# Laying out the softmax statistics directly behind the last join of a weight pair

## The chip, the cores and the metric

The kernel runs on one core of a Trainium2 chip. The metric is the time of one execution on the device in microseconds (us), the median of several runs. Engines are named as in the profile: PE is TensorE (matrix products; PEld its weight loads), DVE is VectorE (elementwise work and reductions), ACT is ScalarE (activations and copies), POOL is GpSimd, SP is SyncE (here a queue for transfers).

## The reference

A trunk of two layers over 512 positions of width 1024, in float32. Layer 0 mixes tokens with dilated attention, layer 1 with causal pooling; a SwiGLU feed-forward part of width 2816 follows each. The change lies in the attention: for each of 8 head slots there are three groups with dilations 1, 4 and 16, each with its own queries, keys and values, and the three outputs are merged by their softmax denominators:

```python
for g, (window, dil) in enumerate(ATTN_PAIRS):          # (128,1), (512,4), (2048,16)
    o, lse = dilated_window_attention(qkv[:, :, g, 0], qkv[:, :, g, 1], qkv[:, :, g, 2], window, dil, slopes[g])
    outs.append(o)
    lses.append(lse)
wts = jax.nn.softmax(jnp.stack(lses, axis=0), axis=0)
o = jnp.sum(wts[..., None] * o, axis=0).reshape(B, S, ATTN_WIDTH)
return o.astype(h.dtype) @ w_out
```

## The kernel before

**Products.** Every float32 product is done in three matmuls with a high and a low part of each factor (`mult`, L391 to L393: weight high by data high, weight high by data low, weight low by data high). Weight matrices come from HBM as raw tiles and are split by ACT (high part, `whi`, L96) and DVE (low part, `wlo`, L97).

**Pairs.** Most weights are taken as a `Pair`: two column blocks whose product is formed with seven half products in place of eight (`seven` for queries, keys and the even heads' values, `values12` for other values). A pair goes through four weight steps: `blocks`, `sums`, `more` (two DVE additions, L173 and L174, then a split) and `last` (a split of a half tile, `halfhi` and `halflo`). The steps of all pairs stand in one queue; `pump` takes the next one if its ring of buffers has room, and issues loads that fit. In `seven` each of the seven products is followed by `behind(i)`, which calls `pump` once and then whatever attention work is registered for that turn in `after[i]`. DVE adds the half products together; the last of these additions, the last join (L446 in `seven`, L594 in `values12`), is put on the list `mark`.

**Heads.** For each head h, `scores0` and `scores12` compute scores and their maxima and sums, the statistics `st` (DVE reductions, and sums that ACT writes beside its exponentials, L667). One group of statistics has its positions in another order across partitions than the other, so `merge` exchanges them: DVE spreads `st` out into the tile `far` (L680, multiplying with the mask `place`), TensorE multiplies it with the matrix `swap` (L684), DVE picks the result apart (L687, L690), and a short chain of small operations ends in the factors `co` for the probabilities. `turn0` and `turn12` transpose the probabilities and `output` multiplies them with the values. This work of head h−1 is spread over the three pairs of head h by `between(h, g)`: `merge(h-1)` stands at turn 2 of the first of them. An even head ends with the values pair that goes through `seven` (tiles `vt`), an odd one with `values12`. The last head has its `merge` at turn 3 of its own `values12`.

**Order.** The program is written as one stream; a planner sets each engine's queue from it before the run: by its own estimate of times, an engine gets, among the instructions that would be ready, the one that stands first in the program. On the chip each engine takes its queue in order. `tc.issue_after(x)` adds that instructions of x's engine within the block come behind x in that queue, without waiting for x to finish. In the kernel before, `merge` uses this to keep `far` behind the most recent last join:

```python
far = apool.tile([P, 4 * NT, NT], F32, tag="b12", name="far")
with tc.issue_after(mark[-1].ins) if mark else nullcontext():
    nc.vector.tensor_mul(far, ...)
```

`far` lives in the buffer of `b12` (the position biases that `scores12` of the same head has read, and that POOL writes anew for the next head, L624). PSUM banks are handed out by `ps()` in a ring of eight (`RING`).

Of the kernel before, what the change touches and what calls it, by code (L numbers as in the profile page):

```python
# [8 lines left out]
F32 = mybir.dt.float32  # L9
# [6 lines left out]
P = 128  # L16
# [11 lines left out]
NT = S // P  # L28
# [23 lines left out]
def trunk(ctx: ExitStack, tc: tile.TileContext, xT, norms, w_first, w_qk, w_qkp, w_v0, w_v0p, w_v12, w_out, w_pair, w_down, w_down0, w_down1, w_down2, w_pin, w_pgrp,  # L52
          consts, ident_in, invcnt_in, outT):
    nc = tc.nc
# [17 lines left out]
    def ps(tag=None):  # L72

        if tag is None:
            if turn["ring"] is None:
                tag = "ps"
            else:
                tag = RING[turn["ring"] % len(RING)]
                turn["ring"] += 1
        return psum.tile([P, S], F32, tag=tag, name=tag, bufs=BANKS[tag])  # L80
# [59 lines left out]
    class Pair:  # L140
# [38 lines left out]
        def last(self):  # L179
            self.made("l", "half", self.c.t, 1)  # L180
            self.c.done()
# [108 lines left out]
    def give(key):  # L290
        free.append(held.pop(key))
# [85 lines left out]
    mark = []  # L377
# [17 lines left out]
    def part(unit, name):  # L395
        while name not in unit.w:
            pump(must=True)
        return unit.w[name]

    def seven(T, one, two, scratch, after={}, blocks=False):  # L400


        unit, = units.popleft()
        into, left, right = by_block if blocks else in_place, slice(0, 1), slice(1, 2)

        def again(v):
            return v.unsqueeze(1).to_broadcast([P, 2, H2])

        p1, p26, p45, p73 = ps(), ps(), ps(), ps()

        def behind(i):
            pump()
            for f in after.get(i, ()):
                f()

        w = part(unit, "b")
        mult(p1[:, :H2], w, 0, T, "11")
        first, sums = scratch("first"), scratch("sums")
        nc.scalar.copy(first[:, :H2], p1[:, :H2])
        behind(0)  # L420
        mult(p26[:, :H2], w, 1, T, "21")
        w.done()
        behind(1)
        w = part(unit, "s")
        mult(p45[:, H2:], w, 0, T, "1")
        behind(2)
        mult(p73[:, :H2], w, 1, T, "3")
        w.done()
        behind(3)
        w = part(unit, "m")  # L430
        mult(p26[:, H2:], w, 0, T, "2")
        nc.vector.tensor_add(into(one), p26, again(first[:, :H2]))
        behind(4)
        mult(p73[:, H2:], w, 1, T, "22")
        w.done()
        if blocks:
            for a in (left, right):
                nc.vector.tensor_add(in_place(sums, a), in_place(p73, a), into(one, right))
        else:
            nc.vector.tensor_add(sums, p73, again(one[:, H2:]))  # L440
        behind(5)
        w = part(unit, "l")
        mult(p45[:, :H2], w, 0, T, "4")
        w.done()
        nc.vector.tensor_sub(into(two), p45, again(sums[:, :H2]))
        mark.append(nc.vector.tensor_sub(into(one, right), sums[:, H2:], p45[:, H2:]))  # L446
        behind(6)

    def chain(T, share, left, right, low, high, behind=None):

# [66 lines left out]
    with tc.tile_pool(name="opool", bufs=1) as opool:  # L517
        early = opool.tile([P, HEADS, S], F32R, tag="o", name="early")
        with tc.tile_pool(name="apool", bufs=1) as apool:
# [4 lines left out]
            A = {}  # L524
# [73 lines left out]
            VT = []  # L598
# [48 lines left out]
            def scores12(h):  # L647
# [19 lines left out]
                    nc.scalar.activation(v, v, AF.Exp, bias=nm[:, 1, r:r + 1], accum_out=st[:, 0, 1, 1, r:r + 1])  # L667
                A[h]["s12"] = s12

            def merge(h):  # L670


                st, s0, s12 = A[h]["st"], A[h]["s0"], A[h]["s12"]
                mx = apool.tile([P, 2, NT], F32, name="mx")
                ex = apool.tile([P, 2, 2, NT], F32, name="ex")
                dd = apool.tile([P, 2, 2, NT], F32, name="dd")
                co = apool.tile([P, 2, NT], F32, name="co")
                far = apool.tile([P, 4 * NT, NT], F32, tag="b12", name="far")
                with tc.issue_after(mark[-1].ins) if mark else nullcontext():
                    nc.vector.tensor_mul(far, st[:, 0].rearrange("p a s b -> p (a s b)").unsqueeze(2).to_broadcast(  # L680
                        [P, 4 * NT, NT]), place[:, None].to_broadcast([P, 4 * NT, NT]))
                p = ps()
                for a in range(2):
                    nc.tensor.matmul(p[:, a * 32:(a + 1) * 32], swap,  # L684
                                     far[:, (1 - a) * 8:(2 - a) * 8].rearrange("p s r -> p (s r)"), start=True, stop=True)

                nc.vector.tensor_mul(far.rearrange("p (q r) b -> p q r b", r=NT),  # L687
                                     p[:, :64].rearrange("p (q b r) -> p q r b", b=NT, r=NT),
                                     place[:, None, None].to_broadcast([P, 4, NT, NT]))
                nc.vector.tensor_reduce(st[:, 1].rearrange("p a s r -> p (a s r)"), far, axis=AX.X, op=OP.add)  # L690
                nc.vector.tensor_max(mx, st[:, 0, :, 0, :], st[:, 1, :, 0, :])
                nc.vector.tensor_sub(ex, st[:, :, :, 0, :], mx[:, None].to_broadcast([P, 2, 2, NT]))
                nc.scalar.activation(ex, ex, AF.Exp)
                nc.vector.tensor_mul(dd, ex, st[:, :, :, 1, :])
                nc.vector.tensor_add(mx, dd[:, 0], dd[:, 1])
                nc.vector.reciprocal(mx, mx)
                nc.vector.tensor_mul(co, ex[:, 0], mx)
                for b in (1, 2, 3, 0):
                    nc.vector.tensor_scalar(s0blk(s0, b), s0blk(s0, b), co[:, 0, b:b + 1], None, op0=OP.mult)
                for r in range(NT):  # L700
                    v = s12[:, r].rearrange("p g k -> p (g k)")
                    nc.scalar.activation(v, v, AF.Copy, scale=co[:, 1, r:r + 1])
# [53 lines left out]
            H, T, o = {}, {}, []  # L756
# [35 lines left out]
            def scratch(name):  # L792
                return apool.tile([P, S], F32, tag="scratch", name=name, bufs=3)
# [11 lines left out]
            for k in range(KC):  # L805
# [5 lines left out]
                s = slice(k % 2 * NF * P, (k % 2 + 1) * NF * P)  # L811
# [17 lines left out]
            def later(f, *a):  # L829
                return lambda: f(*a)  # L830

            def between(h, g):

                if g == 0:
                    return {2: [later(merge, h - 1)], 4: [later(turn_values, h - 1)] if h > 1 else []} if h % 2 else {
                        1: [later(output, h - 2)], 2: [later(merge, h - 1)]}
                if g == (2 if h == 1 else 1):
                    return {0: [later(turn0, h - 1)], 2: [later(turn12, h - 1)], 4: [later(scores0, h)]}
                return {} if h % 2 else {2: [later(output, h - 1)]}
# [8 lines left out]
            place = apool.tile([P, NT], F32, name="place")  # L848
            nc.sync.dma_start(place, consts[:, 5 * P:])
            VT[:] = [scratch("vt") for c in range(2)]  # L850
            for c in range(2):
                p = product(0)
# [6 lines left out]
            for h in range(1, HEADS):  # L859
                for g in range(3):  # L860
                    if h == 1 and g < NSOLO:
                        for c in range(2):
                            evac(h, 2 * g + c, product(0))
                        for fs in between(h, g).values():
                            for f in fs:
                                f()
                    else:
                        for c in range(2):
                            QKV[h, g, c] = apool.tile([P, S], F32, name=f"qk{g}{c}")
                        seven(T, QKV[h, g, 0], QKV[h, g, 1], scratch, between(h, g), g == 0)  # L870
                if h == 1:
                    whole = opool.tile([P, HEADS, S], F32, tag="o", name="o")
                    o.extend(whole[:, h, :] for h in range(HEADS))
                if h == HEADS - 1:
                    for key in [key for key in held if key[0] == "t"]:
                        give(key)
                    X[:] = [x_tile(k) for k in range(KC)]
                    for k in range(KC):
                        nc.gpsimd.dma_start(X[k], xT[:, k, :])
                if h % 2 == 0:  # L880
                    VT[:] = [apool.tile([P, S], F32, tag=tag, name="vt") for tag in ("row", "o0")]
                    seven(T, *VT, scratch, {0: [later(scores12, h)]}, True)
                elif h < HEADS - 1:
                    QKV[h // 2, 12, 2] = values12({0: [later(scores12, h)]})
                else:
                    QKV[h // 2, 12, 2] = values12({0: [later(scores12, h)], 1: [later(halve, 0), later(halve, 1)],
                                                   2: [later(halve, 2), later(halve, 3)], 3: [later(merge, h)],
                                                   4: [later(halve, 4), later(halve, 5)]})
            for k in range(KC):
                give(("h", k))  # L890
# [1 line left out]
            last = HEADS - 1  # L892
# [478 lines left out]
```

## Time and profile before

| | |
|---|---|
| time, median of 3 runs | 1255.39 us (1254.78 to 1256.69) |
| time of the profiled execution | 1255.31 us |
| its span, first to last instruction | 1253.5 us |
| granted TensorE clock | 0.998 |
| TensorE busy | 1238.3 us (99%) |
| VectorE busy | 1012.8 us (81%) |
| ScalarE busy | 679.9 us (54%) |
| DMA, mean over the span | 151 GB/s |

The times of rows are microseconds from the start of the span. A row of a timeline has the start, the duration, the engine, the line, the operation, the tile written and the tiles read, the shapes and the count; in brackets stands how long the engine was idle before it and what ended that. A row of the waits has the waiting instruction, the instruction that it waited for, the total in us, the number of times and the longest. A row of the windows has the stretch and its length, then the busy time of each engine with its number of instructions, the granted clock, the share of DMA time and GB/s. The attention heads' part that the change touches lies between about 60 and 440 us; the feed-forward part, the pooling layer and the second feed-forward part follow.

### The profile page before, as it was taken

To read this page: it belongs to the slowest core of one execution; us is meant where nothing else is said; L and a number is where in the kernel's file an instruction comes from. 1 tells how busy PE (TensorE), PEld (TensorE's weight loads), DVE (VectorE), ACT (ScalarE), POOL (GpSimd) and SP (SyncE) were. 2 spreads that over 40 slices of the span, in tenths; PEclk is the share of its full clock that TensorE was granted. 3 is DMA by queue.
4 is the path that set the end of the run, shared out by engine and by line. 5 is a ranking of instruction groups with operands and counts; after the bars stand their busy time and mean duration, and the time that the engine had idled before them with its cause. 6 is when DMAs were issued, how large, how long until landed. Compare 5 with 4: busy or idle time off the path is not lost. (4 is left out here: it accounts for less than half of the span.)

```text
span 1253.5 us, 23247 instructions
## 1 busy us (share of the span) xinstructions
PE 1238.3 (99%) x9072; PEld 1173.6 (94%) x9072; DVE 1012.8 (81%) x1687; ACT 679.9 (54%) x1171; POOL 157.7 (13%) x147
## 2 busy tenths in 40 slices
PE   9999999999999999999999999999999999999997
PEld 7889999999999998889999999988788999999997
DVE  7987787878778747698778888798989877888876
ACT  6444554445455535466466556554446646656652
POOL 1111111111111010101111111100220111111100
PEclk9999999999999999999999999999999999999999
DMA  8336556655755443437777687553144777677742
GB/s 280 109 92 171 136 143 149 165 133 146 186 141 140 138 152 119 109 94 184 184 186 170 177 191 178 137 198 123 51 118 100 190 189 179 147 192 205 169 123 68
DMA packets 76719, 189.91 MB, mean 151 GB/s; under 512 B 7600, under 2 KB 15936, under 8 KB 76608
## 3 DMA queue, kind: packets, MB, share of 16 engines
q1 hardware_dynamic: 51696, 142.26, 35.8%
q0 software_dynamic: 24336, 45.63, 22.2%
q8 instruction: 71, 1.16, 0.4%
q10 hardware_dynamic: 576, 0.52, 0.1%
q14 instruction: 40, 0.33, 0.1%
HBM read 186.29 MB, written 2.10 MB: 150 GB/s over the span
## 5 line engine op out<-in xcount | busy, mean ns | idle before, releaser
L96 ACT ACTIVATE whi<-raw 128x1024 fp32r<-128x1024 f32 (+2 forms) x315 | 318.7, 1016 | 254.0 <-PE seed L392 78.5
L97 DVE TENSOR_TENSOR wlo<-raw,whi 128x1024 fp32r<-128x1024 f32 (+2 forms) x315 | 366.6, 1167 | 108.0 <-ACT whi L96 107.2
L158 POOL DMA_DIRECT2D raw<-w_pair x34 | 41.1, 1209 | 312.3 <-DMA raw<-w_pair 61.9
L391 PE MATMUL sum<-tt,whi 128*128 128x256 f32 x272 | 77.0, 283 | 1.6 <-ACT seed L473 0.8
L392 PE MATMUL sum<-tt,whi 128*128 128x256 f32 x272 | 76.6, 282 | 0.0
L393 PE MATMUL sum<-tt,wlo 128*128 128x256 f32 x272 | 76.4, 281 | 0.0
L96 ACT ACTIVATE halfhi<-rawhalf 128x512 fp32r<-128x512 f32 (+1 forms) x87 | 53.1, 612 | 19.5 <-PE sum L392 12.2
L173 DVE TENSOR_TENSOR raw<-raw 128x512 f32<-128x512 f32 (+1 forms) x87 | 57.5, 661 | 1.8 <-issue 1.7
L174 DVE TENSOR_TENSOR raw<-raw 128x512 f32<-128x512 f32 (+1 forms) x87 | 57.5, 661 | 0.2
L97 DVE TENSOR_TENSOR halflo<-rawhalf,halfhi 128x512 fp32r<-128x512 f32 (+1 forms) x87 | 57.4, 661 | 0.0
L158 POOL DMA_DIRECT2D raw<-w_down x24 | 28.9, 1206 | 213.8 <-DMA raw<-w_down 75.4
L391 PEld LDWEIGHTS sum<-tt,whi 128*128 128x128 f32 x272 | 51.3, 189 | 2.0 <-ACT seed L473 1.0
L473 ACT COPY seed<-sum 128x256 f32<-128x256 f32 x58 | 20.8, 359 | 57.5 <-PE sum L393 56.3
L392 PEld LDWEIGHTS sum<-tt,whi 128*128 128x128 f32 x272 | 51.3, 188 | 0.0
L393 PEld LDWEIGHTS sum<-tt,wlo 128*128 128x128 f32 x272 | 51.2, 188 | 0.0
L391 PE MATMUL sum<-hz,whi 128*128 128x256 f32 x160 | 45.3, 283 | 0.5 <-ACT seed L473 0.3
L392 PE MATMUL sum<-hz,whi 128*128 128x256 f32 x160 | 45.2, 283 | 0.0
L392 PE MATMUL seed<-hy,whi 128*128 128x256 f32 x160 | 45.2, 282 | 0.0
L393 PE MATMUL seed<-hy,wlo 128*128 128x256 f32 x160 | 45.1, 282 | 0.0
L393 PE MATMUL sum<-hz,wlo 128*128 128x256 f32 x160 | 45.1, 282 | 0.0
L391 PE MATMUL seed<-hy,whi 128*128 128x256 f32 x160 | 45.0, 281 | 0.0
L158 POOL DMA_DIRECT2D raw<-w_qkp x18 | 22.0, 1222 | 166.9 <-DMA raw<-w_qkp 109.4
(610 smaller groups left out, 4628.3 us busy)
## 6 DMA issues: line engine op xcount, KB each, us to landing
raw<-w_pair SPq DMA_DIRECT2D x78, 512.0 KB, 4.8
raw<-w_qkp SPq DMA_DIRECT2D x36, 512.0 KB, 4.3
raw<-w_pair POOLq DMA_DIRECT2D x34, 512.0 KB, 7.7
raw<-w_down SPq DMA_DIRECT2D x32, 384.0 KB, 3.7
raw<-w_v SPq DMA_DIRECT2D x18, 512.0 KB, 4.0
raw<-w_qkp POOLq DMA_DIRECT2D x18, 512.0 KB, 7.3
rawhalf<-w_pair SPq DMA_DIRECT2D x34, 256.0 KB, 4.5
raw<-w_down SPq DMA_DIRECT2D x16, 512.0 KB, 4.7
```

The lines of the kernel that those rows point to most:

```text
L96: nc.scalar.activation(hi, v, AF.Copy)
L97: nc.vector.tensor_tensor(lo, v, hi.bitcast(F32), op=OP.subtract)
L158: nc.gpsimd.dma_start(b.rearrange("p (a c) -> p a c", a=2), self.src[:, None, 3 * q:].to_broadcast([P, 2, q]), accum_op=OP.add)
L173: nc.vector.tensor_add(a[:, :q], a[:, :q], b[:, :q])
L174: nc.vector.tensor_add(a[:, q:2 * q], a[:, q:2 * q], a[:, :q])
L391: nc.tensor.matmul(dst, w.t[0][:, c], th, start=k == 0 and not onto, stop=False, skip_group_check=onto)
L392: nc.tensor.matmul(dst, w.t[0][:, c], tl, start=False, stop=False, skip_group_check=onto)
L393: nc.tensor.matmul(dst, w.t[1][:, c], th, start=False, stop=k == n - 1, skip_group_check=onto)
L473: nc.scalar.copy(e, c)
```

## The change

The making of `far` is taken out of `merge` into a function of its own, `lay(h)`, still behind the most recent last join. `merge` takes the tile from `A[h]`. `lay` is called at these places:
- even heads 2, 4 and 6: inside `seven` of the head's values pair, after the last join and before `behind(6)`; the DVE instructions that this `behind(6)` issues are put behind `far`;
- odd heads 1, 3 and 5: at turn 0 of the next head's first pair, two turns before `merge`;
- head 0: directly before its `merge`;
- head 7: at turn 2 of `values12`, ahead of two `halve` calls, one turn before its `merge`.

```diff
-    def seven(T, one, two, scratch, after={}, blocks=False):
+    def seven(T, one, two, scratch, after={}, blocks=False, last=None):
...
         mark.append(nc.vector.tensor_sub(into(one, right), sums[:, H2:], p45[:, H2:]))
-        behind(6)
+        if last:
+            with tc.issue_after(last().ins):
+                behind(6)
+        else:
+            behind(6)
...
+            def lay(h):
+
+                st = A[h]["st"]
+                far = A[h]["far"] = apool.tile([P, 4 * NT, NT], F32, tag="b12", name="far")
+                with tc.issue_after(mark[-1].ins) if mark else nullcontext():
+                    return nc.vector.tensor_mul(far, st[:, 0].rearrange("p a s b -> p (a s b)").unsqueeze(2).to_broadcast(
+                        [P, 4 * NT, NT]), place[:, None].to_broadcast([P, 4 * NT, NT]))
+
             def merge(h):
-                st, s0, s12 = A[h]["st"], A[h]["s0"], A[h]["s12"]
+                st, s0, s12, far = (A[h][name] for name in ("st", "s0", "s12", "far"))
...
-                far = apool.tile([P, 4 * NT, NT], F32, tag="b12", name="far")
-                with tc.issue_after(mark[-1].ins) if mark else nullcontext():
-                    nc.vector.tensor_mul(far, ...)
...
                 if g == 0:
-                    return {2: [later(merge, h - 1)], 4: [later(turn_values, h - 1)] if h > 1 else []} if h % 2 else {
-                        1: [later(output, h - 2)], 2: [later(merge, h - 1)]}
+                    return {0: [later(lay, h - 1)] if h == 1 else [], 2: [later(merge, h - 1)],
+                            4: [later(turn_values, h - 1)] if h > 1 else []} if h % 2 else {
+                        0: [later(lay, h - 1)], 1: [later(output, h - 2)], 2: [later(merge, h - 1)]}
...
-                    seven(T, *VT, scratch, {0: [later(scores12, h)]}, True)
+                    seven(T, *VT, scratch, {0: [later(scores12, h)]}, True, later(lay, h))
...
-                                                   2: [later(halve, 2), later(halve, 3)], 3: [later(merge, h)],
+                                                   2: [later(lay, h), later(halve, 2), later(halve, 3)], 3: [later(merge, h)],
```

More of the change, by code (lines that the diff above doesn't have):

```diff
@@ L677, in merge @@
                 co = apool.tile([P, 2, NT], F32, name="co")
-                far = apool.tile([P, 4 * NT, NT], F32, tag="b12", name="far")
-                with tc.issue_after(mark[-1].ins) if mark else nullcontext():
-                    nc.vector.tensor_mul(far, st[:, 0].rearrange("p a s b -> p (a s b)").unsqueeze(2).to_broadcast(
-                        [P, 4 * NT, NT]), place[:, None].to_broadcast([P, 4 * NT, NT]))
                 p = ps()
```

## The prediction

> **What bounds the kernel now.** I read the page first, for the busiest engine; then the waits of TensorE, for what still holds it; then the line of the moved instruction with who waited for it; then the timelines around its eight places.
>
> ```profile
> span 1253.5 us, 23247 instructions
> ...
> PE 1238.3 (99%) x9072; PEld 1173.6 (94%) x9072; DVE 1012.8 (81%) x1687; ACT 679.9 (54%) x1171; POOL 157.7 (13%) x147
> ...
> PE 31%; DVE 2%; ACT 0%; issue 0%; POOL 0%; DVEq 0%
> ```
>
> TensorE is busy for 1238.3 of 1253.5 us and makes up nearly all of the chain that ended last. So only time in which TensorE stands still can be won; a microsecond of VectorE (DVE) counts only where TensorE waits for it.
>
> ```profile
> engine line waited for: us in total, times, longest us
> PE ps L684 <- DVE far L680: 2.1, 3, 0.8
> PE seed L804 <- DVE idle L801: 1.2, 1, 1.2
> ```
>
> The longest entry among TensorE's waits is the exchange matmul of `merge` (L684) waiting for the layout `far` (L680), the very instruction that the change moves. It waits three times out of eight. In the stretch with the attention heads nothing else is lost:
>
> ```profile
> core 0: us, PE busy (x) PEld busy (x) DVE busy (x) ACT busy (x) POOL busy (x), PEclk, DMA share, GB/s
> ...
> 60.00:440.00 380.00, 377.87 (x3030) 370.86 (x3029) 304.97 (x483) 193.31 (x352) 55.07 (x55) 1.00 0.58 144
> ```
>
> 380.00 − 377.87 is 2.13 us, just those three waits, at a granted clock of 1.00.
>
> **Why it waits: the queue of DVE.** The first of the three places (head 2), DVE's timeline, and ACT's for the statistics:
>
> ```profile
> 169.95 1.11 DVE L445 TENSOR_TENSOR vt<-ps,sums 128x512 f32<-128x512 f32 x1
> 170.89 0.65 DVE L446 TENSOR_TENSOR vt<-sums,ps 128x256 f32<-128x256 f32 x1
> 171.37 0.69 DVE L173 TENSOR_TENSOR raw<-raw 128x512 f32<-128x512 f32 x1
> 171.98 0.68 DVE L97 TENSOR_TENSOR halflo<-rawhalf,halfhi 128x512 fp32r<-128x512 f32 x1
> 172.58 0.68 DVE L174 TENSOR_TENSOR raw<-raw 128x512 f32<-128x512 f32 x1
> 173.18 0.22 DVE L680 TENSOR_TENSOR far<-st,place 128x64 f32<-128x64 f32 x1
> 174.12 0.23 DVE L687 TENSOR_TENSOR far<-ps,place 128x64 f32<-128x64 f32 x1 [0.72 <-PE ps L684]
> ...
> 174.72 1.22 DVE L97 TENSOR_TENSOR wlo<-raw,whi 128x1024 fp32r<-128x1024 f32 x1
> ...
> 165.43 0.19 ACT L667 ACTIVATION_READ_ACCUMULATOR s<-s,nm 128x1 f32 x1
> ```
>
> The statistics were complete at 165.62, and the last join (L446) began at 170.89. What stood between it and `far` are three operations of two weight steps (`more`: L173 and L174; `last`: L97). They start at 171.37; without them `far` could start there, 173.18 − 171.37 = 1.81 us sooner.
>
> TensorE at this place, then at a place where it does not wait (head 1), then at heads 4 and 6:
>
> ```profile
> 172.37 0.28 PE L393 MATMUL ps<-tx,wlo 128*128 128x256 f32 x1
> 172.49 0.28 PE L391 MATMUL seed<-t,whi 128*128 128x256 f32 x1
> 173.45 0.63 PE L684 MATMUL ps<-far,const 128*128 128x32 f32 x4 [0.68 <-DVE far L680]
> ...
> 174.12 0.28 PE L393 MATMUL seed<-t,wlo 128*128 128x256 f32 x1
> ...
> 123.36 0.28 PE L393 MATMUL seed<-tx,wlo 128*128 128x256 f32 x1
> 123.48 0.53 PE L684 MATMUL sum<-far,const 128*128 128x32 f32 x4
> ...
> 124.17 0.28 PE L393 MATMUL sum<-t,wlo 128*128 128x256 f32 x1
> ...
> 282.27 0.28 PE L393 MATMUL seed<-tx,wlo 128*128 128x256 f32 x1
> ...
> 283.44 0.60 PE L684 MATMUL ps<-far,const 128*128 128x32 f32 x4 [0.77 <-DVE far L680]
> ...
> 284.08 0.28 PE L393 MATMUL sum<-t,wlo 128*128 128x256 f32 x1
> ...
> 392.23 0.28 PE L393 MATMUL seed<-tx,wlo 128*128 128x256 f32 x1
> ...
> 393.31 0.63 PE L684 MATMUL ps<-far,const 128*128 128x32 f32 x4 [0.68 <-DVE far L680]
> ...
> 393.98 0.28 PE L393 MATMUL sum<-t,wlo 128*128 128x256 f32 x1
> ```
>
> **The change part by part.** *Heads 2, 4, 6: `far` right behind the join.* Between the two L393 rows of a place lie the same instructions everywhere: the exchange and two product matmuls. Where there is no wait this takes 124.17 − 123.36 = 0.81 us from start to start. With the wait it takes 1.75 (head 2), 1.81 (head 4) and 1.75 (head 6). The differences are 0.94, 1.00 and 0.94, in sum 2.88 us. The recorded idle sums to less, 2.13, because a matmul's row reaches 0.28 us after its start while the next one normally starts 0.12 later (172.37, 172.49): the row's overhang of 0.16 is hidden in "busy", and the exchange itself is 0.60 to 0.63 long after a wait instead of 0.53. I take starts, 2.88.
> The Trainium skill speaks to this choice (Perfetto Trace Analysis, Per-instruction lifecycle, Tensor Engine Instruction): the start of a matmul's row is the beginning of its data fetch, and its end is only estimated from its size. By that rule starts may be subtracted and ends may not, so 2.88 rather than 2.13; the trace agrees as far as the three places exceed the fourth by more than the recorded idle.
>
> *What is late next.* TensorE would reach the exchange at 172.49 (in the program it stands ahead of that L391; the planner put one matmul before it only because `far` was late). By then `far` has ended at 171.37 + 0.22 = 171.59, 0.9 us ahead. The PSUM bank of the exchange is, eight turns of the ring back, that of the pair's last product, which L446 reads until 171.54; also 0.95 ahead. So no second wait is found, and the whole 2.88 should come back.
>
> *What `far` displaces.* The three weight operations and their ScalarE (ACT) half start later by what `far` takes in DVE's queue. From start to start that is 0.13 us:
>
> ```profile
> 117.23 0.69 DVE L97 TENSOR_TENSOR halflo<-rawhalf,halfhi 128x512 fp32r<-128x512 f32 x1
> 117.83 0.22 DVE L680 TENSOR_TENSOR far<-st,place 128x64 f32<-128x64 f32 x1
> 117.96 0.69 DVE L173 TENSOR_TENSOR raw<-raw 128x512 f32<-128x512 f32 x1
> ...
> 183.36 1.11 DVE L445 TENSOR_TENSOR qk<-ps,sums 128x512 f32<-128x512 f32 x1
> ...
> 175.31 0.28 PE L391 MATMUL sum<-t,whi 128*128 128x256 f32 x1
> ```
>
> Cover: the weights that `more` makes (low part done at 174.72 + 1.22 = 175.94) belong to the pair after the running one. The running pair reads its own at 175.31, the next one about a join's distance later, 183.36 − 169.95 = 13.4 us, so near 188.7: about 12.8 us of lead against 0.13. I cost it at nothing; without that lead it would be 0.13 for each of the three, 0.4 us. The exchange's results (L687 onward) come about 0.9 us sooner and fill the 0.72 us for which DVE stood idle.
>
> *Holding the step behind the join (`behind(6)` under `issue_after`).* Following the step queue through the code, at the joins of these three heads no weight step is drawn there: the `sums` step is drawn at `behind(5)`, `more` and `last` one and two turns into the next pair. So the hold binds nothing on DVE here; what moves `far` is its new place in the program, which gives it precedence. Loads that the step may issue sit on the SP and POOL queues; `lay` issues no transfer and passes none.
>
> *Heads 1, 3, 5.* `far` goes into `behind(0)`, after that turn's step. At head 1 it already starts at 117.83, behind the last weight operation of the pair, while its exchange starts at 123.48; the lead of 5.4 us makes any shift there worth nothing; heads 3 and 5 stand in the same order. *Head 0*: `lay` stands directly before `merge`, as now. *Head 7*: `lay` moves one turn ahead of `merge`, past steps and two `halve` calls; no TensorE wait stands there to be won.
>
> **Sum.** The profiled execution takes 1255.31 us, 1.8 more than its span and 0.08 below the median of the runs, 1255.39. 1255.31 − 2.88 = 1252.43; from the median, 1252.5, which I predict (−0.23%). About 0.2% (2.5 us) is what a measurement of this kernel can tell from no change, so the forecast lies just beyond it.
>
> **The rivals.** *Only part returns.* If a start is delayed by something else by the overhang, only the recorded 2.13 returns: 1253.3. Against it stand the four start-to-start counts.
>
> *Nothing returns: the wait was not `far`'s.* If the exchange waits for its PSUM bank or its weights, or the planner leaves `far` where it is, the time stays 1255.4. For it: the same bubble at the same spot three times. Against it: the exchange starts at 173.45 and `far` ends at 173.40, and the bank's last reader ends 1.9 us before that. In a sentence of its own: the Trainium skill (Perfetto Trace Analysis, Optimization Strategy) says that a gap that recurs on the engine that should be saturated can mean that SBUF or PSUM is too short for the next tile. By it the time would be the 1255.4 of this rival; the trace has another releaser by name, so I give it little.
>
> *Slower: at head 7 `far` blocks DVE.* There the statistics are late:
>
> ```profile
> 432.13 2.35 DVE L97 TENSOR_TENSOR wlo<-raw,whi 128x1024 fp32r<-128x1024 f32 x2
> 434.75 0.23 DVE L680 TENSOR_TENSOR far<-st,place 128x64 f32<-128x64 f32 x1 [0.27 <-ACT s L667]
> ...
> 437.52 0.28 PE L550 MATMUL ps<-wlo,t 128*128 128x256 f32 x1
> ```
>
> With more precedence `far` may be queued ahead of both weight splits and hold them until 434.75: they would run 0.23 + 434.75 − 432.13 = 2.85 us later, the first (half of 2.35) ending near 436.2. TensorE reads it from 437.52, so 1.3 us of cover are left and the price is nothing. From a hold of some 4.2 us on, each further one goes to TensorE in full; at 4.2 + 2.88 + 2.5 = 9.6 us the kernel is slower than now by over 0.2%. There the time would be 1255.4 + 2.5 = 1257.9. Little speaks for so long a hold.
>
> **How the numbers follow.** Forecast 0.66, own range 1251.5 to 1253.5 (0.4 us for the displaced steps, and the runs shown differ by 1.9). Partial 0.15, none 0.14, slower 0.05. Faster by over 0.2% means under 1252.9: 0.7 of the forecast (0.46), a third of the partial case, and a trifle of the third, 0.53. Slower: 0.04. Same: 0.43. The range, 1251.4 to 1254.8, holds the forecast and the partial case, and leaves out most of "nothing returns" and the slower case.
>
> **What the changed profile would show.** The TensorE wait of L684 for `far` gone from the list, TensorE's idle in the attention stretch near zero; `far` of heads 2, 4 and 6 starting right behind its join, ahead of L173; 0.81 us between the L393 rows on both sides of the exchange; the exchange ahead of the L391 that now precedes it. Everything later should simply stand 2.9 us earlier. The prediction is wrong if another wait of TensorE appears in the list, for instance of a product for `wlo` at head 7, or in the feed-forward part where the planner may order things anew, or if `far` moves and the gap stays.

## The result and the profile after

The kernel with the change takes 1252.16 us (median of 12 runs, 1250.33 to 1254.04), the one before 1254.97 us in the same sitting (12 runs, 1254.13 to 1256.81). The ratio is 0.9976, 95% interval 0.9969 to 0.9983: faster by 2.8 us, 0.24%. Predicted were 1252.5 us and a gain of 2.88.

The page of the profiled execution (1251.78 us) and the waits of TensorE:

```profile
span 1250.0 us, 23243 instructions
...
PE 1237.6 (99%) x9072; PEld 1174.0 (94%) x9072; DVE 1013.6 (81%) x1687; ACT 679.7 (54%) x1171; POOL 154.9 (12%) x147
```

```profile
engine line waited for: us in total, times, longest us
PE seed L812 <- DVE idle L809: 1.2, 1, 1.2
PE sum L391 <- ACT seed L477: 1.1, 2, 0.8
```

The number of busy instructions of every engine is the same; the four fewer in the first line are of the kinds that are not counted as busy. The wait of the exchange matmul for `far`, which headed the list, is gone (the exchange is now L692, `far` L679). The stretch with the attention heads, by windows:

```profile
core 0: us, PE busy (x) PEld busy (x) DVE busy (x) ACT busy (x) POOL busy (x), PEclk, DMA share, GB/s
...
60.00:440.00 380.00, 380.00 (x3058) 373.78 (x3058) 308.67 (x492) 193.79 (x352) 54.22 (x58) 1.00 0.59 146
```

TensorE is busy in all of the 380 us, where 2.13 were missing. The first of the three places, head 2, in the timelines of VectorE and TensorE:

```profile
169.71 0.65 DVE L446 TENSOR_TENSOR vt<-sums,ps 128x256 f32<-128x256 f32 x1
170.19 0.23 DVE L679 TENSOR_TENSOR far<-st,place 128x64 f32<-128x64 f32 x1
170.31 0.68 DVE L173 TENSOR_TENSOR raw<-raw 128x512 f32<-128x512 f32 x1
170.91 0.69 DVE L97 TENSOR_TENSOR halflo<-rawhalf,halfhi 128x512 fp32r<-128x512 f32 x1
171.51 0.69 DVE L174 TENSOR_TENSOR raw<-raw 128x512 f32<-128x512 f32 x1
172.11 0.22 DVE L695 TENSOR_TENSOR far<-ps,place 128x64 f32<-128x64 f32 x1
...
176.31 0.16 DVE L705 TENSOR_TENSOR co<-ex,mx 128x8 f32<-128x8 f32 x1
```

```profile
122.31 0.53 PE L692 MATMUL sum<-far,const 128*128 128x32 f32 x4
...
171.19 0.28 PE L393 MATMUL ps<-tx,wlo 128*128 128x256 f32 x1
171.31 0.53 PE L692 MATMUL ps<-far,const 128*128 128x32 f32 x4
171.67 0.36 PE L391 MATMUL seed<-t,whi 128*128 128x256 f32 x1
...
171.99 0.28 PE L393 MATMUL seed<-t,wlo 128*128 128x256 f32 x1
...
432.91 0.53 PE L692 MATMUL sum<-far,const 128*128 128x32 f32 x4
```

`far` stands between the last join and L173, ends at 170.42, and TensorE starts the exchange at 171.31 straight behind its last product, without a bracket for idle time. Between the L393 rows on both sides lie 171.99 − 171.19 = 0.80 us; there were 1.75.

One measure serves for all that follows: the stretch from the exchange of head 1 to that of head 7. It was 436.96 − 123.48 = 313.48 us and is 432.91 − 122.31 = 310.60 us, 2.88 less. Outside of it the two executions differ too, for reasons that were not followed: the one after reaches the exchange of head 1 already 1.17 us sooner, and needs 0.55 longer from that of head 7 to the end. Hence the span is shorter by 3.5 and not by 2.9. The times alone, with their interval of 2.1 to 3.9 us for the gain, would not tell 2.88 from 2.13.

### The profile page after: what moved, and what is told of

Its sections match the earlier page's. It is cut to its first block, busy times and chain, and to the rows that moved or that the text cites. A ratio compares the mean times of both kernels' runs of the same rounds, so it can differ in the third digit from the quotient of the medians.

```text
span 1250.0 us, 23243 instructions
## 1 busy us (share of the span) xinstructions
PE 1237.6 (99%) x9072; PEld 1174.0 (94%) x9072; DVE 1013.6 (81%) x1687; ACT 679.7 (54%) x1171; POOL 154.9 (12%) x147
## 5 line engine op out<-in xcount | busy, mean ns | idle before, releaser
L393 PE MATMUL sum<-tt,wlo 128*128 128x256 f32 x272 | 76.5, 281 | 0.0
L173 DVE TENSOR_TENSOR raw<-raw 128x512 f32<-128x512 f32 (+1 forms) x87 | 57.6, 662 | 2.1 <-issue 2.0
L174 DVE TENSOR_TENSOR raw<-raw 128x512 f32<-128x512 f32 (+1 forms) x87 | 57.7, 663 | 0.2
L393 PEld LDWEIGHTS sum<-tt,wlo 128*128 128x128 f32 x272 | 51.2, 188 | 0.0
L393 PE MATMUL seed<-hy,wlo 128*128 128x256 f32 x160 | 45.2, 283 | 0.0
L393 PE MATMUL sum<-hz,wlo 128*128 128x256 f32 x160 | 45.2, 283 | 0.0
```

Of the source, the lines that this page charges most:

```text
L173: nc.vector.tensor_add(a[:, :q], a[:, :q], b[:, :q])
L174: nc.vector.tensor_add(a[:, q:2 * q], a[:, q:2 * q], a[:, :q])
L393: nc.tensor.matmul(dst, w.t[1][:, c], th, start=False, stop=k == n - 1, skip_group_check=onto)
```

## The experiments

Each was timed against the kernel before on the same chip. "Stretch" is the measure above, from the profiled execution.

**The new place without the call in the pair and without the hold.** Every head's layout is registered at turn 0 of the next pair; `seven` is as before the change.

```diff
-    return {0: [later(lay, h - 1)] if h == 1 else [], 2: [later(merge, h - 1)], ...
+    return {0: [later(lay, h - 1)], 2: [later(merge, h - 1)], ...
...
-    seven(T, *VT, scratch, {0: [later(scores12, h)]}, True, later(lay, h))
+    seven(T, *VT, scratch, {0: [later(scores12, h)]}, True)
```

> The layout of every head is registered at turn 0 of the next head's first pair, with no call inside the pair and no hold on the step behind the join. Theory (place in the program ahead of the steps `more` and `last` is all that matters): the same queues as after the change, 310.6 us from the exchange of head 1 to that of head 7 (before 313.5), 1252.2 us. Rival (the hold on the step behind the join does part of the work): above 310.6, up to 313.5, 1253 to 1255.

Measured: 1252.48 us against 1255.28, ratio 0.9980 (0.9971 to 0.9988); stretch 434.32 − 123.72 = 310.60 us. The queues of the engines are, instruction by instruction, those after the change. So the place in the program does it all; the hold on the step behind the join does nothing here.

**Only the other heads.** Heads 2, 4 and 6 keep the layout in `merge`; the rest is as after the change.

```diff
-    seven(T, *VT, scratch, {0: [later(scores12, h)]}, True, later(lay, h))
+    seven(T, *VT, scratch, {0: [later(scores12, h)]}, True)
...
 def merge(h):
+    if "far" not in A[h]:
+        lay(h)
```

> Only heads 0, 1, 3, 5 and 7 get the new place; heads 2, 4 and 6 keep the layout inside merge. Theory (the three waits are the whole gain): 313.5 us between the exchanges, three TensorE waits of 0.7 us for the layout, 1255.0 us. Rival (part of the gain comes from the other heads): less than 313.5, 1253 to 1254.5.

Measured: 1255.62 us against 1255.28, ratio 1.0002 (0.9994 to 1.0011); stretch 436.26 − 122.77 = 313.49 us. Its waits of TensorE begin with the old one:

```profile
PE ps L694 <- DVE far L679: 2.1, 3, 0.8
```

The gain lies in the three even heads alone.

**How late may `far` be?** The last join of heads 2, 4 and 6 is computed again (same operands, same result) ahead of `far`, once or twice.

```diff
 mark.append(nc.vector.tensor_sub(into(one, right), sums[:, H2:], p45[:, H2:]))
 if last:
+    for i in range(1):            # the other kernel: range(2)
+        mark.append(nc.vector.tensor_sub(into(one, right), sums[:, H2:], p45[:, H2:]))
     with tc.issue_after(last().ins):
```

> At heads 2, 4, 6 the last join is computed once more (same result) ahead of the layout; the planner also puts one weight addition (L173) there, so the layout comes about 0.6 + 0.5 = 1.1 us later than after the change, TensorE's queue unchanged. Theory (TensorE loses only what the layout is late for its slot, 0.9 us of lead): late by about 0.25, with the restart 0.35 a place, 311.6 us between the exchanges, 1253.2 us. Rival (any delay of the layout costs in full): 3.3 us, 313.9 and 1255.5. Rival (the lead is larger than the rows say): 310.6 and 1252.2.

> As the kernel with one repeated join, with two: the planner puts L173 and L174 between them, so the layout comes 2.2 us later than after the change, and two product matmuls stand ahead of the exchange in TensorE's queue. Theory (a place costs what the layout is late for its slot, plus 0.1 us): 1.1 us late, 1.2 a place, 314.1 us between the exchanges of heads 1 and 7, that is slower than before the change in this stretch (313.5); some 1255.7 to 1256.5 us. Rival (the wait hides work that comes back elsewhere): 313.0 or less.

Measured with one: stretch 435.39 − 123.67 = 311.72 us, time 1255.05 us against 1255.28 (ratio 0.9998, 0.9990 to 1.0007). With two: stretch 436.54 − 122.55 = 313.99 us, time 1256.41 us against 1255.57 (1.0011, 1.0002 to 1.0020). VectorE at head 2 with one repeated join, then TensorE there with one and with two:

```profile
171.07 0.65 DVE L446 TENSOR_TENSOR vt<-sums,ps 128x256 f32<-128x256 f32 x1
...
172.60 0.22 DVE L681 TENSOR_TENSOR far<-st,place 128x64 f32<-128x64 f32 x1
```

```profile
172.55 0.28 PE L393 MATMUL ps<-tx,wlo 128*128 128x256 f32 x1
172.97 0.60 PE L694 MATMUL ps<-far,const 128*128 128x32 f32 x4
173.40 0.36 PE L391 MATMUL seed<-t,whi 128*128 128x256 f32 x1
```

```profile
171.67 0.28 PE L392 MATMUL seed<-t,whi 128*128 128x256 f32 x1
172.80 0.63 PE L694 MATMUL ps<-far,const 128*128 128x32 f32 x4 [0.85 <-DVE far L681]
173.26 0.36 PE L393 MATMUL seed<-t,wlo 128*128 128x256 f32 x1
```

From the matmul ahead of the exchange to the one behind it 0.48 us pass after the change (171.19 to 171.67). Here it is 0.85 with one join and 1.59 with two, 0.37 and 1.11 more. The exchange starts 0.30 and 1.01 us behind its slot (0.12 us behind the matmul ahead of it). Before the change it was 173.45 − 172.49 − 0.12 = 0.84 late and cost 0.94. So each place costs its lateness and 0.07 to 0.10 us more for the restart. With one join `far` starts 172.60 − 171.07 = 1.53 us behind the start of the first join, after the change 170.19 − 169.71 = 0.48. Of these 1.05 us of delay 0.30 reached the exchange, so the usable lead is some 0.75 us and not the 0.9 between the rows. The row of the exchange with one join has no bracket although 0.37 us were lost: a missing bracket is no proof that nothing was lost. The stretches came out within 0.1 us of the expected ones. The time with one join did not: 1253.2 was expected, and its interval, 1254.0 to 1256.2, leaves that out. It was run again.

> The kernel with one repeated join once more: its stretch between the exchanges was 311.7 us, 1.8 below that before the change, and its median only 0.2 below. Theory (the rest of the kernel scatters by more than a microsecond from run to run, and the median of 12 runs had a high draw): again 311.7, and a median near 1253.5. Rival (the repeated join costs some 1.3 us outside of the stretch): again 1255.0.

Measured: stretch 434.04 − 122.33 = 311.71 us again; 1254.40 us against 1255.57, ratio 0.9992 (0.9983 to 1.0001). This lies between the two theories, and its interval, 1253.4 to 1255.7 us, holds both their times (1253.5 and 1255.0), so it decides nothing. The stretch gained 1.8 us both times, the whole time 0.2 and 1.2. Where the other 1.5 and 0.6 us went stays open: no profile of this kernel shows a wait that would be its own, and outside of the stretch its two profiled executions take 941.7 and 940.7 us, those of the other kernels 938.7 to 941.6.

**Is the PSUM bank the second bound?** `far` stays early, but the last join, which reads the bank of the pair's last product, is repeated four times behind it.

```diff
-    with tc.issue_after(last().ins):
+    far = last().ins
+    for i in range(4):
+        with tc.issue_after(far):
+            mark.append(nc.vector.tensor_sub(into(one, right), sums[:, H2:], p45[:, H2:]))
+        far = mark[-1].ins
+    with tc.issue_after(far):
         behind(6)
```

> The layout stays directly behind the last join at heads 2, 4, 6, but the last join, which reads the pair's last product, is computed four times more behind it, with weight operations in between; the last one ends some 4 us after the layout. TensorE's queue up to the exchange is unchanged. Theory (the exchange also needs the PSUM bank of the pair's last product, eight turns of the ring back): TensorE waits until that end, 3.0 us a place, 319.7 us between the exchanges, 1261.3 us. Rival (only the layout holds the exchange, the bank is another one): 310.6 and 1252.2.

Measured: 1262.82 us against 1255.28, ratio 1.0057 (1.0042 to 1.0071); stretch 443.69 − 123.48 = 320.21 us. The time is close to what the theory gave, but by luck: the reason is another one, and the theory is wrong. The rows of VectorE, of TensorE, the waits, and a window behind the longest of them:

```profile
171.36 0.22 DVE L684 TENSOR_TENSOR far<-st,place 128x64 f32<-128x64 f32 x1
...
174.73 0.63 DVE L451 TENSOR_TENSOR vt<-sums,ps 128x256 f32<-128x256 f32 x1
...
176.33 0.20 DVE L700 TENSOR_TENSOR far<-ps,place 128x64 f32<-128x64 f32 x1
...
183.81 0.16 DVE L710 TENSOR_TENSOR co<-ex,mx 128x8 f32<-128x8 f32 x1
...
184.47 1.06 DVE L712 TENSOR_SCALAR s<-s,co 128x256 f32<-128x256 f32 x4
```

```profile
172.48 0.53 PE L697 MATMUL ps<-far,const 128*128 128x32 f32 x4
...
184.86 0.70 PE L724 MATMUL seed<-ident,s 128*128 128x128 f32 x4 [1.55 <-DVE s L712]
```

```profile
PE seed L735 <- ACT s L715: 5.2, 2, 3.5
...
PE seed L724 <- DVE s L712: 1.6, 1, 1.6
...
PE sum L665 <- DVE qk L445: 0.6, 1, 0.6
```

```profile
407.20:411.00 3.80, 3.80 (x22) 3.80 (x23) 0.89 (x4) 2.21 (x5) 0.91 (x1) 0.64 0.40 141
```

The exchange starts at 172.48 and its successor follows at once, while the last repeated join still reads the product until 175.36. So the exchange does not use that bank. What costs the time is the next link: VectorE, with 4 joins more and the weight operations set among them, picks up the exchanged statistics at 176.33 and has the factors `co` at 183.81, 11.3 us behind the start of the exchange (5.0 after the change), and the transposes of the scaled probabilities wait for them, 1.6 and 5.2 us. The stretch is 9.6 us longer than after the change; with the 0.6 for a join (L445) 7.4 of them are recorded waits. Part of the rest is the clock: in the 3.8 us behind the longest wait, 3.5 us at head 6, the granted clock was 0.64, which by an estimate from these two numbers costs 3.8 × 0.36 = 1.4 us. The remaining 0.8 was not followed. The waits of 0.7 to 0.8 us before the change left the clock at 1.00 over the stretch.

**The slower rival.** At head 7 `far` is put ahead of exactly the two weight splits in VectorE's queue (`weight` is set where whole weight tiles are split).

```diff
+    hold = []
     def split(hi, lo, v, weight=False):
         nc.scalar.activation(hi, v, AF.Copy)
+        with tc.issue_after(hold[0]) if hold and weight else nullcontext():
             nc.vector.tensor_tensor(lo, v, hi.bitcast(F32), op=OP.subtract)
...
-    1: [later(halve, 0), later(halve, 1)], 2: [later(lay, h), later(halve, 2), later(halve, 3)], 3: [later(merge, h)],
+    1: [later(halve, 0), later(halve, 1), lambda: hold.append(lay(h).ins)],
+    2: [later(halve, 2), later(halve, 3)], 3: [hold.clear, later(merge, h)],
```

> At head 7 the layout is put ahead of exactly the two weight splits (wlo) that now precede it in VectorE's queue, which then stand still until the statistics of that head are there; the rest as after the change. Theory (1.3 us of cover are left, as the prediction has it): no TensorE wait there, 310.6 us between the exchanges, 1252.2 us. Rival (the prediction's slower case): TensorE waits for wlo at the product behind the exchange of head 7, which stands 1 to 3 us later; 1253 to 1255 us.

Measured: 1252.86 us against 1255.57, ratio 0.9978 (0.9969 to 0.9987); stretch 433.12 − 122.52 = 310.60 us.

```profile
430.90 0.23 DVE L682 TENSOR_TENSOR far<-st,place 128x64 f32<-128x64 f32 x1 [2.53 <-ACT s L674]
431.05 2.35 DVE L100 TENSOR_TENSOR wlo<-raw,whi 128x1024 fp32r<-128x1024 f32 x2
```

```profile
433.68 0.28 PE L557 MATMUL ps<-wlo,t 128*128 128x256 f32 x1
```

VectorE stands still for 2.53 us with both splits behind it, and TensorE loses nothing: the first split ends near 432.2 (half of the row) and is read at 433.68. Holds long enough to use up this cover were not tried.

## Why the prediction was right, and where it was not

*The sum.* 2.88 us were taken from the starts of rows at the three places, and the stretch became shorter by 2.88. The recorded idle of 2.13 would have been too little: the rival "only part returns" falls. The count by starts and the stretch agree here to 0.01 us. That fits what the Trainium skill (Perfetto Trace Analysis, Per-instruction lifecycle, Tensor Engine Instruction) states: the end of a matmul's row is an estimate and not a measurement.

*The mechanism.* `far` waited behind the weight operations of VectorE's queue, and the exchange behind `far`. Shown by the rows after, by the kernel that leaves only the even heads at the old place and has all the loss, by the one that gives them the early place in another way and has none, and by the delays that bring the loss back.

*The hold.* That it binds nothing was read from the order of the steps; the kernel without it has the same queues.

*The displaced weight steps.* L173 starts 0.12 us behind `far`'s start (0.13 was taken), and no wait of TensorE for weights is in the list. Four joins of displacement showed none either.

*What is late next: two weak steps without effect on the sum.* First, the bank. The prediction had the exchange's bank free 0.95 us ahead of need, as that of the pair's last product; it is another one, as the four late joins showed. So the times it gave for that bank's last reader prove nothing, there and against the rival "nothing returns". The rows agree with the count of turns in the tag, `ps`, of which there are three banks; which of them the exchange takes was not read out. Second, the link behind the exchange. The prediction said only that its results come about 0.9 us sooner, and did not ask whether that is soon enough for who reads them. Before the change, at head 2:

```profile
180.09 0.16 DVE L697 TENSOR_TENSOR co<-ex,mx 128x8 f32<-128x8 f32 x1
...
180.70 1.08 DVE L699 TENSOR_SCALAR s<-s,co 128x256 f32<-128x256 f32 x4
```

```profile
181.94 0.60 PE L711 MATMUL seed<-ident,s 128*128 128x128 f32 x4
```

The row of VectorE merges four instructions and ends at 181.78, 0.16 us ahead of the transposes (L711). That is not the spare time, since the first transposes need only the first of the four: with the four late joins they begin at 184.86, while the merged row runs from 184.47 to 185.53. By this distance of 0.39 the ones of head 2 could have begun near 181.09, so about 0.8 us were to spare. The other three parts are made, and needed, one after the other in about the same steps. With TensorE 0.94 to 1.00 sooner, 0.1 to 0.2 us of each place would have come back there if VectorE had kept its times; this is an estimate from the rows.

VectorE did not keep them. The exchange's results came 0.84 us sooner (L687 at 174.12, L695 at 172.11, less the 1.17 by which this execution runs ahead), close to the 0.9 of the prediction, and `co` 2.6 us sooner (180.09, 176.31). The order is new: the small operations now stand ahead of a join (L432) and of a weight step (L173, L174) that used to go among them. Why the planner chose this order was not examined.

*Heads 0, 1, 3, 5 and 7.* No effect, as predicted; the place of their `far` in VectorE's queue is unchanged. The slower rival at head 7 did not come about, and where it was forced its price was nothing, with some 1.4 us of cover left (predicted 1.3).

## What to carry to other kernels

A small instruction that another engine waits for should get its precedence when its inputs are ready and not where its consumer stands in the program: 0.2 us of work behind 1.8 us of work without haste cost 0.94 us a time. Measure such a wait from start to start against a place without the wait, and then follow the chain one link further, to whoever reads the result; the spare time there decides whether the gain stays. Read it per instruction: a merged row ends later than the part of it that is needed first. Where the whole gain is a few microseconds in a thousand, a stretch between two marks in the trace tells it to 0.01 us, while whole times need a dozen runs.

## What had not been expected

Outside of the attention stretch single executions differ by more than what was sought. The exchange of head 1 came between 122.31 and 123.72 us in these profiles, and from the exchange of head 7 to the end it took 816.2 (1249.3 − 433.12, head 7 held) to 818.4 us (1252.4 − 434.04, one join again) although the queues there are the same. Part of it is a wait in the feed-forward parts that was 3.1 us in one execution (the kernel without call and hold) and 0.8 in the profile after the change, with the same queues:

```profile
PE sum L391 <- ACT seed L465: 3.1, 3, 1.7
```

```profile
PE sum L391 <- ACT seed L469: 0.8, 2, 0.7
```

What sets it was not tried. The stretch itself repeated to 0.01 us: 310.60 in three kernels.
